# Reordering one DMA queue in a planned attention stage: small moves ahead of bulk loads, residual tiles behind the bias, and other bank tags

## The chip, the cores and the metric

The kernel runs on one core of one Trainium2 chip. The metric is device time in microseconds (us); lower is better. Engines: TensorE (PE), VectorE (DVE), ScalarE (ACT), GpSimd (POOL), and SyncE (SP), which here only issues DMAs.

## The reference, cut to what matters

A two-layer bidirectional encoder is applied to two groups of tokens, 512 and 256 long, 768 columns in all, with a model width of 1024. Layer 0 mixes tokens by windowed attention (16 query heads, 4 key heads, blocks of 128 queries, a bias from relative positions, a sink logit per head):

```
qkv = h @ w_qkv
logits = einsum('bqgrd,bkgd->bgrqk', qb, kb) * scale + band_bias
m = max(max(logits), sink);  p = exp(logits - m)
probs = p / (sum(p) + exp(sink - m))
x = x + einsum('bgrqk,bkgd->bqgrd', probs, vb) @ w_o
```

Layer 1 mixes by a short gated convolution. After each mixer follow an MLP with squared ReLU, `x + square(relu(h @ w_up)) @ w_down`, and a gated per-layer input, `x + (p[i] @ w_proj) * sigmoid(norm(x) @ w_gate)`. All is float32. The change lies in the attention of layer 0 and in the output projection after it.

## The kernel before, in words

**Products.** Every float32 product is made of three reduced ones: an operand is split into a high part (ScalarE, a rounding copy) and a low part (VectorE, the rest), and high by high, high by low and low by high are summed in PSUM. So each weight block that is loaded into a `wraw` tile is first split by ScalarE (`whi`, L656 in the attention) and VectorE (`wlo`, L660).

**Attention is one list.** `mixer_attention` doesn't issue instructions as it goes. It registers operations (`op`, `first`) with an engine, a cost, what must be finished before (`after`), what must merely have started before (`behind`), and for a DMA the time that its bytes take on a modelled pipe. `Plan.order` then plays this list on the host: five engines with a clock of their own, at each step the engine that can start earliest, and on it, among the operations that are ready, the one with the largest `reach` (the modelled time from it to the end) plus a bonus. Scores and what follows them have a bonus of 10 (`URGENT`) on PE, so other products fill the gaps between them. SP also waits when eight DMAs are under way (`LANES`). An operation is offered only when all that it depends on has been placed. The order that comes out is emitted as it stands, one instruction stream for each engine; on the chip an engine works its stream in order and waits where data is late, whatever the planner thought.

**What goes over SP's queue in attention.** Loads of weights (`fetched`: w_q, w_k, w_v, w_o, the projection and p of layer 1), the residual tiles `xa` (x once more, one tile of 128 x 768 for each of 8 output blocks, `load_part`), stores of a small projection (`pj`), and three kinds of moves:
- query moves: `queries` computes two heads for each of 8 units; ScalarE makes the high part `qh` (L712) and VectorE the low part `ql` (L715), and for each head two DMAs copy the halves into a tile `q` that stacks high and low parts over the 128 partitions. The scores S (L1086, L1087) of the head need both;
- key moves, the same for the keys (`kk<-qh`, `kk<-ql`);
- bias moves: for each of 4 groups of heads, two tiles of four moves each, from a skewed table in DRAM (`load_bias`, `bias<-skew`). Four such tiles exist, so those of group 3 wait until group 1 has read its own.

All DMA issues of the list come from L631. Units 4 and 5 are the queries of group 2, 6 and 7 those of group 3.

**Order around the change.** Groups 0 to 3 are attended one after the other, 6 blocks of 128 queries and 4 heads each: score, reduce with the bias (L1093, VectorE), exponent (L1103, ScalarE), scale, transpose (L1129), split, times the values (O, L1144), join into `heads`. Beside them PE works the query products of the units to come and, once two groups are done, blocks of the output projection (`output_part`, mm<-aos, L680), which VectorE adds into `xa` (L1197). Where the list ends, the rest of the output projection runs in plain order over the 8 output blocks (`PAIRED`, L132), in PSUM banks that `both` draws from a pool with three tags: A (4 banks), B and C (2 each). Without a tag, `fresh` walks the tags in the order C, A, B, A.

Of the kernel before, what the change touches and what calls it, by code (L numbers as in the profile page):

```python
# [50 lines left out]
def trunk_kernel(ctx: ExitStack, tc: tile.TileContext, a: dict, out: bass.AP):  # L51
# [67 lines left out]
    def both(name="mm", tag=None):  # L119

        return [t[:, :H] for t in fresh(name, 2, tag)]
# [348 lines left out]
    class Op:  # L470
        def __init__(self, engine, cost, run, after, behind, tail):
            self.engine, self.cost, self.run, self.tail = engine, cost, run, tail
            self.after, self.behind = after, behind
            self.start = self.reach = None

    class Plan:


        LATE = 6.0
        LANES = 8  # L480
        OWN = {"PE": 0.0, "ACT": 0.13, "DVE": 0.12, "POOL": 0.1, "SP": 0.0}
        OTHER = {"PE": 0.22, "ACT": 0.15, "DVE": 0.14, "POOL": 0.3, "SP": 0.1}

# [53 lines left out]
        def order(self):  # L537
            after = {id(o): 0 for o in self.ops}
            nexts = {id(o): [] for o in self.ops}
            for o in self.ops:  # L540
                for d in o.after + o.behind:
                    nexts[id(d)].append(o)
                after[id(o)] = len(o.after) + len(o.behind)
            known, sorted_ = dict(after), [o for o in self.ops if after[id(o)] == 0]
            for o in sorted_:
                for n in nexts[id(o)]:
                    known[id(n)] -= 1
                    if known[id(n)] == 0:
                        sorted_.append(n)
            for o in reversed(sorted_):  # L550
                tail = o.tail + self.LATE if o.tail is not None else self.OTHER[o.engine]
                o.reach = o.cost + max((n.reach + (tail if o in n.after else 0.0) for n in nexts[id(o)]), default=0.0)
            free = {e: 0.0 for e in self.OWN}
            waiting = {e: [] for e in self.OWN}
            pipe, landings = 0.0, [0.0] * self.LANES

            def offer(o):
                o.ready = max(
                    [self.done(d, o.engine) for d in o.after] + [d.start for d in o.behind], default=0.0
                )  # L560
                waiting[o.engine].append(o)

            for o in self.ops:
                if after[id(o)] == 0:
                    offer(o)
            out = []
            while any(waiting.values()):
                best = None
                for e, os in waiting.items():
                    if os:  # L570
                        t = max(free[e], min(o.ready for o in os), landings[-self.LANES] if e == "SP" else 0.0)
                        o = max((o for o in os if o.ready <= t), key=lambda o: o.reach + o.bonus)
                        if best is None or t < best[0]:
                            best = t, o
                t, o = best
                waiting[o.engine].remove(o)
                o.start = t
                free[o.engine] = t + o.cost
                if o.tail is not None:
                    pipe = max(pipe, t + o.cost + 1.3) + o.tail  # L580
                    o.landed = pipe + 0.3
                    landings.append(o.landed)
                o.seq = len(out)
                out.append(o)
                for n in nexts[id(o)]:
                    after[id(n)] -= 1
                    if after[id(n)] == 0:
                        offer(n)
            assert len(out) == len(self.ops)
            return out  # L590
# [12 lines left out]
    def mixer_attention():  # L603
# [23 lines left out]
        def dma(box, src, n, after=(), uses=(), queue="SP", rate=400e3):  # L627

            def run():
                d, s = src()  # L630
                (nc.sync if queue == "SP" else act).dma_start(d, s)  # L631

            lands = n / rate
            if box is not None and box.op is None:
                return first(box, queue, 0.46, run, after, uses, lands)
            return op(queue, 0.46, run, after, uses, lands=lands)

        def fetched(src):
            n = src.shape[1]
            raw = new("wraw", 3, lambda: wp.tile([P, CH], F32, name="wraw", bufs=3))  # L640
            raw.n = n
            raw.landed = [dma(raw, lambda: (raw.t[:, :n], src), P * 4 * n, uses=())]
            return raw

        def pair_tiles():
# [4 lines left out]
        def prepared(raw, n):  # L650

            w, m = pair_tiles(), raw.n
            w.raw = raw.landed[0]

            def high():
                act.activation(w.t[0][:, :m], raw.t[:, :m], AF.Copy)  # L656
                w.parts = blocks(w.t[0][:, :m], n), blocks(w.t[1][:, :m], n)

            def low():
                dve.tensor_tensor(w.t[1][:, :m], raw.t[:, :m], w.t[0][:, :m].bitcast(F32), ALU.subtract)  # L660

            hi = first(w, "ACT", A(m), high, [raw.landed], [raw.key])
            lo = op("DVE", V(m), low, [hi], [w.key, raw.key])
            w.ready = [hi, lo]
            w.keys = [w.key]
            return w
# [194 lines left out]
        for m in range(KB):  # L861
            t = new("L", BL, lambda: odd.tile([P, 2 * LW], F32, tag="L", name="L", bufs=BL)[:, :T])
# [30 lines left out]
        for o, n in ((0, W0), (W0, SEQS[1])):  # L893
            ps = bank("S", "ss")
# [144 lines left out]
        biases = {}  # L1039
# [19 lines left out]
        xa = {}  # L1059
# [124 lines left out]
                ops = split_op(hi, lo, lambda i=i: heads[g].t[:, i, :], T, hparts[g], [heads[g].key])  # L1184
                aos[2 * g + i] = block_of(hi, lo, ops)

        def load_part(ms):
            for m in ms:
                xa[m] = place(m, "xa", F32)
                xa[m].ready = [dma(xa[m], lambda m=m: (xa[m].t[:], a["x"][m]), 393216)]  # L1190

        def output_part(m, w, n, col=0):
            ops = []
            for ps, o, e, last in halves(w, [aos[k] for k in range(n)], ("mm0", "mm1"), col):

                def run(ps=ps, o=o, e=e):
                    dve.tensor_tensor(xa[m].t[:, o : o + e], xa[m].t[:, o : o + e], ps.t[:, :e], ALU.add)  # L1197

                op("DVE", V(e), run, [last, xa[m].ready], [ps.key, xa[m].key])
# [7 lines left out]
        def second_projected():  # L1207
            ps = [pair(2 + p, "p1", F32R) for p in range(2)]
            part1 = []
            for k in range(2):  # L1210
                raw = fetched(a["p"][1, :, k, :])

                def high(k=k, raw=raw):
                    act.activation(ps[0].t[:, k, :], raw.t[:, :T], AF.Copy)

                def low(k=k, raw=raw):
                    dve.tensor_tensor(ps[1].t[:, k, :], raw.t[:, :T], ps[0].t[:, k, :].bitcast(F32), ALU.subtract)

                if k == 0:
                    h = first(ps[0], "ACT", A(T), high, [raw.landed], [raw.key])  # L1220
                    l = first(ps[1], "DVE", V(T), low, [h], [raw.key, ps[0].key])
                else:
                    h = op("ACT", A(T), high, [raw.landed, h], [raw.key, ps[0].key])
                    l = op("DVE", V(T), low, [h, l], [raw.key, ps[0].key, ps[1].key])
                b = Box()
                b.parts = lambda k=k: [p.t[:, k, :] for p in ps]
                b.ready, b.keys = [h, l], [p.key for p in ps]
                part1.append(b)
            w = prepared(fetched(a["proj"][1, 0]), 2)
            for m in range(KB // 2):  # L1230
                projected(1, m, w, part1, temp("n", "pjs"), ("mm0",), False)

# [13 lines left out]
        load_bias(3)  # L1246
        split_heads(0)
        split_heads(1)
        load_part(range(4))
        group_of_heads(2)  # L1250
        for j in range(2):
            w = prepared(fetched(a["w_o0"][j]), 4)
            for i in range(2):
                output_part(2 * j + i, w, 4, i * P)
        split_heads(2)
        load_part(range(4, KB))
        group_of_heads(3)
        for m in range(4, KB):
            output_part(m, prepared(fetched(a["w_o1"][m - 4]), 6), 6)
        split_heads(3)  # L1260
        with s1:
            with tc.manual_schedule(engines={ET.Activation, ET.PE, ET.DVE, ET.SP, ET.Pool}):
# [4 lines left out]
    xa, aos = mixer_attention()  # L1267
# [1054 lines left out]
    behind, product, w0 = second_inputs(xs0[24:])  # L2322
    w = [weight(a["w_o0"][2], 4)] * 2
    w2 = weight(a["w_o2"], 2, tag="z")
    for i, m in enumerate(PAIRED):
        if i == 1:
            w += [weight(a["w_o0"][3], 4)] * 2
        ps = both()
        if m < KB // 2:
            group2(ps, terms_of(w[m], [p[4:] for p in aos], col=m % 2 * P))  # L2330
        else:
            group2(ps, terms_of(w2, [p[6:] for p in aos], col=(m - 4) * P))
        add(m, ps, xa[m])
        n1.block(m, x(m))
        behind(i)
# [103 lines left out]
```

## Time and profile before

| what | us |
|---|---|
| median of 3 runs (lowest, highest) | 1646.12 (1645.8, 1646.88) |
| the profiled execution | 1647.11 |
| its span, first to last instruction | 1645.3 |
| TensorE busy in it | 1627.5 |
| VectorE busy | 1389.8 |
| ScalarE busy | 920.7 |

The span is that of the instructions; the execution's own time is 1.81 longer, and durations below are all from this one execution. Rows of an engine in order of time give the start, the duration, engine, line, output and input, and in brackets how long the engine sat idle just before and what released it. SPq rows are DMA issues, xN is how many were merged, and their duration is the time in which they were issued. Rows of DMA issues by line end with the size of each and the median time from issue to landing. Rows of a stretch give its length, the busy time of PE, PE's weight loads, VectorE, ScalarE and GpSimd, the granted clock of PE as a share of full speed, the busy share of the DMA engines, and GB/s.

### The profile page before, as it was taken

Reading aid. Unit: us, or ns where it says so; the run is one execution under the profiler, and the core shown is the slowest. Engines: PE = TensorE matmul, PEld = TensorE weight load, DVE = VectorE, ACT = ScalarE, POOL = GpSimd, SP = SyncE. Lnnn points to the kernel's source line nnn. Section 1 sums busy time; section 2 is a strip of 40 time slices with the busy share of each in tenths; the row PEclk is TensorE's granted clock in tenths of the full one; section 3 lists DMA queues with packets and bytes.
Section 4 is the critical chain, followed back from the end, with each engine's and each line's share of the span. In section 5 each row is a group of like instructions: output and inputs, shape, how many; then the busy total and the mean of one; then the engine's idle time right before and its main releaser. Section 6 shows DMA issues by size and latency. Waiting matters only on the chain.

```text
span 1645.3 us, 24138 instructions
## 1 busy us (share of the span) xinstructions
PE 1627.5 (99%) x9371; PEld 1575.4 (96%) x9371; DVE 1389.8 (84%) x2212; ACT 920.7 (56%) x1458; POOL 12.3 (1%) x60
## 2 busy tenths in 40 slices
PE   9999999999999999999999999999999999999998
PEld 7988889999999999999999999999999999999987
DVE  7578987999899989977878888769989989999686
ACT  7378884765555545545654344555545555655465
POOL 0000000000000000000000000000000000000000
PEclk9999999999999999999999999999999999999999
DMA  8745303222221222232311222211222222222332
GB/s 309 193 131 135 107 26 96 93 75 74 68 77 66 76 65 85 70 93 78 116 61 52 77 77 77 78 52 53 76 67 85 67 68 74 78 67 75 118 97 87
DMA packets 47822, 144.80 MB, mean 88 GB/s; under 512 B 6075, under 2 KB 9531, under 8 KB 47708
## 3 DMA queue, kind: packets, MB, share of 16 engines
q1 hardware_dynamic: 47708, 143.27, 27.8%
q8 instruction: 73, 1.20, 0.3%
q14 instruction: 41, 0.34, 0.1%
HBM read 123.85 MB, written 9.96 MB: 81 GB/s over the span
## 4 chain that ended last, share of the span: by engine, by line
PE 90%; DVE 5%; DMA 2%; ACT 2%; issue 1%; SPq 0%; DVEq 0%; POOL 0%; ACTq 0%; POOLq 0%
PE a L464 32%; PE b L464 8%; PE mm L132 8%; PE mm L680 8%; PE d L464 5%; PE c L464 5%; PE p L1474 4%; PE gate L1811 4%; PE B L464 4%; PE C L464 4%; PE gate L132 2%; PE down L1811 2%; PE pt L1129 1%; PE O L1144 1%; PE S L1086 1%
## 5 line engine op out<-in xcount | busy, mean ns | idle before, releaser
L432 ACT ACTIVATE whi<-sum 128x1024 fp32r<-128x1024 f32 x66 | 70.2, 1063 | 253.4 <-PE a L464 251.7
L464 PE MATMUL a<-xs,whi 128*128 128x384 f32 x608 | 118.0, 335 | 1.3 <-DVE y L1592 1.3
L464 PEld LDWEIGHTS a<-xs,whi 128*128 128x128 f32 x608 | 106.4, 188 | 2.3 <-DVE y L1592 2.0
L464 PE MATMUL b<-t,zhi 128*128 128x384 f32 x528 | 106.7, 334 | 0.0
L464 PE MATMUL a<-t,zhi 128*128 128x384 f32 x528 | 106.6, 334 | 0.0
L464 PE MATMUL a<-t,whi 128*128 128x384 f32 x528 | 106.6, 334 | 0.0
L1633 DVE TENSOR_TENSOR x<-x,a 128x384 f32<-128x384 f32 x112 | 62.1, 554 | 51.3 <-PE a L464 51.2
L464 PE MATMUL a<-act,whi 128*128 128x384 f32 x448 | 95.6, 334 | 0.0
L464 PEld LDWEIGHTS a<-t,whi 128*128 128x128 f32 x528 | 92.9, 188 | 0.0
L464 PEld LDWEIGHTS b<-t,zhi 128*128 128x128 f32 x528 | 92.9, 188 | 0.0
L464 PEld LDWEIGHTS a<-t,zhi 128*128 128x128 f32 x528 | 92.9, 188 | 0.0
L432 ACT ACTIVATE zhi<-sum 128x1024 fp32r<-128x1024 f32 x66 | 69.8, 1058 | 38.5 <-DVE sum L408 32.7
L443 DVE TENSOR_TENSOR wlo<-wraw,whi 128x1024 fp32r<-128x1024 f32 x72 | 87.6, 1217 | 0.0
L432 ACT ACTIVATE whi<-wraw 128x1024 fp32r<-128x1024 f32 x72 | 75.7, 1051 | 19.3 <-issue 15.6
L680 PE MATMUL mm<-xs_mix,whi 128*128 128x512 f32 (+1 forms) x320 | 81.4, 341 | 0.0
L443 DVE TENSOR_TENSOR zlo<-sum,zhi 128x1024 fp32r<-128x1024 f32 x66 | 80.3, 1217 | 0.5 <-ACT zhi L432 0.5
L443 DVE TENSOR_TENSOR wlo<-sum,whi 128x1024 fp32r<-128x1024 f32 x66 | 80.4, 1218 | 0.0
L464 PEld LDWEIGHTS a<-act,whi 128*128 128x128 f32 x448 | 79.3, 188 | 0.0
L464 PE MATMUL a<-xs,wlo 128*128 128x384 f32 x304 | 64.9, 334 | 0.0
L464 PE MATMUL b<-t,zlo 128*128 128x384 f32 x264 | 61.1, 335 | 0.7 <-DVE zlo L443 0.7
L464 PE MATMUL a<-t,zlo 128*128 128x384 f32 x264 | 60.9, 334 | 0.0
L464 PE MATMUL a<-t,wlo 128*128 128x384 f32 x264 | 60.9, 334 | 0.0
(391 smaller groups left out, 4480.2 us busy)
## 6 DMA issues: line engine op xcount, KB each, us to landing
wraw<-in_up SPq DMA_DIRECT2D x64, 512.0 KB, 3.4
wraw<-in_down SPq DMA_DIRECT2D x64, 512.0 KB, 3.5
wraw<-in_w_in SPq DMA_DIRECT2D x24, 512.0 KB, 3.4
wraw<-in_gate SPq DMA_DIRECT2D x16, 512.0 KB, 3.5
wraw<-in_w_q SPq DMA_DIRECT2D x8, 512.0 KB, 6.2
wraw<-in_w_out SPq DMA_DIRECT2D x8, 512.0 KB, 3.6
x_in<-in_x SPq DMA_DIRECT2D x8, 384.0 KB, 6.9
pj<-L SPq DMA_DIRECT2D x8, 384.0 KB, 5.7
```

What stands on the lines that cost most here:

```text
L132: pe.matmul(t, lhsT=w, rhs=x[:, o:e], start=first and i == 0 and j == 0, stop=last and i == n - 1 and j == 2)
L432: act.activation(hi[:], src, AF.Copy)
L443: dve.tensor_tensor(lo[:], src, hi[:].bitcast(F32), ALU.subtract)
L464: pe.matmul(ps, lhsT=a, rhs=b, start=start and i == 0, stop=i == len(terms) - 1, skip_group_check=True)
L680: pe.matmul(ps.t[:, :n], lhsT=a_, rhs=b_, start=k == 0 and j == 0, stop=k == len(xs) - 1 and j == 2,)
L1086: pe.matmul(S.t[:, :w], lhsT=q, rhs=khh_[g].t[:, kk], start=True, stop=False)
L1129: pe.transpose(pt.t[:, h * P : (h + 1) * P], lg[h // 2].t[:, h % 2, 1 + b * P : 1 + (b + 1) * P], ident[:],)
L1144: pe.matmul(O.t[:], lhsT=vb, rhs=part.t[:], start=b == 0 and i == 0, stop=b == nk - 1 and i == 1)
L1474: pe.matmul(ps[i][o], lhsT=wt[:, c], rhs=xs[f"x{h + 1}{1 + o}"][m][part], start=k == 0 and j == 0, stop=k == KB - 1 and j == 2,)
L1633: dve.tensor_tensor(t[:, o : o + H], t[:, o : o + H], f, op)
L1811: pe.matmul(ps.t[:, o : o + n], lhsT=a_, rhs=b_, start=begin and i == 0 and j == 0, stop=end and i == len(terms) - 1 and j == 2,)
```

## The change

1. Operations get a flag `bulk`. It is set on the loads of p and of the projection of layer 1, on the loads of w_o (`w_o0`, `w_o1`) and on the residual tiles. When the planner would start a bulk operation on SP and another one there, not bulk, is ready within `HOLD` = 2.0 us, it takes the one of these that is ready first, and SP waits for it.
2. The residual tiles 0 to 3 must start behind the last bias move of group 3.
3. The output projection after the list takes its banks by the tags B, A, C, A in turn, not by the walk C, A, B, A.

```diff
@@ class Op / class Plan
-            self.after, self.behind = after, behind
+            self.after, self.behind, self.bulk = after, behind, False
...
         LANES = 8
+        HOLD = 2.0
@@ Plan.order
                         o = max((o for o in os if o.ready <= t), key=lambda o: o.reach + o.bonus)
+                        if o.bulk:
+                            soon = [u for u in os if not u.bulk and u.ready <= t + self.HOLD]
+                            if soon:
+                                o = min(soon, key=lambda u: u.ready)
+                                t = max(t, o.ready)
                         if best is None or t < best[0]:
                             best = t, o
@@ mixer_attention
-        def fetched(src):
+        def fetched(src, bulk=False):
...
+            raw.landed[0].bulk = bulk
             return raw
...
-        def load_part(ms):
+        def load_part(ms, behind=()):
             for m in ms:
                 xa[m] = place(m, "xa", F32)
                 xa[m].ready = [dma(xa[m], lambda m=m: (xa[m].t[:], a["x"][m]), 393216)]
+                xa[m].ready[0].bulk = True
+                xa[m].ready[0].behind.extend(behind)
...
-                raw = fetched(a["p"][1, :, k, :])
+                raw = fetched(a["p"][1, :, k, :], True)
...
-            w = prepared(fetched(a["proj"][1, 0]), 2)
+            w = prepared(fetched(a["proj"][1, 0], True), 2)
...
-        load_part(range(4))
+        load_part(range(4), biases[3][1].ready[-1:])
         group_of_heads(2)
         for j in range(2):
-            w = prepared(fetched(a["w_o0"][j]), 4)
+            w = prepared(fetched(a["w_o0"][j], True), 4)
...
         for m in range(4, KB):
-            output_part(m, prepared(fetched(a["w_o1"][m - 4]), 6), 6)
+            output_part(m, prepared(fetched(a["w_o1"][m - 4], True), 6), 6)
@@ after attention
-        ps = both()
+        ps = both(tag="BACA"[i % 4])
```

## The prediction

> **What bounds the kernel now.** I read the page first, then who waited for whom on TensorE in the first 420 us (attention and what follows it; the diff touches nothing later), then TensorE in order of time around each wait, then the DMA queue of SyncE (SP) beside it, and last a table of stretches for the granted clock and the DMA rate.
>
> ```profile
> span 1645.3 us, 24138 instructions
> PE 1627.5 (99%) x9371; PEld 1575.4 (96%) x9371; DVE 1389.8 (84%) x2212; ACT 920.7 (56%) x1458; POOL 12.3 (1%) x60
> PE S L1086 <- DMA q<-ql: 4.0, 3, 2.3
> PE mm L132 <- DVE xa L1197: 0.6, 1, 0.6
> 153.45 0.40 PE L1144 MATMUL O<-pl,vv 128*128 128x512 f32 x1
> 156.11 0.35 PE L1086 MATMUL S<-kk,q 128*128 128x256 f32 x1 [2.27 <-DMA q<-ql]
> 167.57 0.36 PE L1086 MATMUL S<-kk,q 128*128 128x256 f32 x1 [0.69 <-DMA q<-ql]
> 207.37 0.39 PE L1086 MATMUL S<-kk,q 128*128 128x256 f32 x1 [1.02 <-DMA q<-ql]
> ```
>
> TensorE (PE) is busy 99% of the span, so the list can only give back PE's own idle time. In attention that is nearly all of one kind: three scores (S) wait 2.27, 0.69 and 1.02 us (4.0 in all) for the low part of their queries, which a DMA copies into place. Everything else PE does there is filler without gaps, and the residue of the projection (L680, then L132) runs on after the last head, so that an idle microsecond saved comes off the end. The next rows are the DMA issues of SP around the three waits, the landing times of a few, and the clock.
>
> ```profile
> 146.46 1.10 SPq L631 DMA_DIRECT2D q<-qh  x2
> 147.65 0.53 SPq L631 DMA_DIRECT2D wraw<-in_w_o  x1
> 148.28 1.10 SPq L631 DMA_DIRECT2D q<-ql  x2
> 149.47 1.08 SPq L631 DMA_DIRECT2D xa<-in_x  x2
> 150.64 10.02 SPq L631 DMA_DIRECT2D bias<-skew  x8
> 160.76 1.11 SPq L631 DMA_DIRECT2D q<-qh  x2
> 161.96 0.54 SPq L631 DMA_DIRECT2D wraw<-in_w_o  x1
> 162.60 1.10 SPq L631 DMA_DIRECT2D q<-ql  x2
> ...
> 201.17 0.54 SPq L631 DMA_DIRECT2D wraw<-in_w_o  x1
> 201.80 1.10 SPq L631 DMA_DIRECT2D q<-ql  x2
> ...
> q<-ql SPq DMA_DIRECT2D x2, 192.0 KB, 7.9
> q<-ql SPq DMA_DIRECT2D x2, 192.0 KB, 5.5
> kk<-ql SPq DMA_DIRECT2D x4, 192.0 KB, 4.2
> ...
> L680 PE MATMUL mm<-aos,whi x160: 277/387/481, 188.1 to 261.6; 128*128 128x512 f32 x80, 128*128 128x256 f32 x80
> L1197 DVE TENSOR_TENSOR xa<-xa,mm x16: 410/548/689, 193.4 to 262.1; 128x512 f32<-128x512 f32 x8, 128x256 f32<-128x256 f32 x8
> ...
> 156.10:157.00 0.90, 0.89 (x6) 0.85 (x7) 0.27 (x1) 0.00 (x0) 0.00 (x0) 1.00 0.95 307
> 157.00:158.00 1.00, 1.00 (x8) 0.90 (x7) 0.65 (x3) 0.90 (x1) 0.00 (x0) 0.69 1.10 224
> 158.00:159.00 1.00, 1.00 (x5) 0.90 (x4) 0.38 (x1) 0.98 (x3) 0.00 (x0) 0.50 1.09 197
> 160.00:161.00 1.00, 1.00 (x6) 0.96 (x5) 1.00 (x2) 1.00 (x5) 0.55 (x1) 0.60 0.44 103
> 161.00:162.00 1.00, 1.00 (x6) 0.82 (x5) 0.96 (x4) 0.60 (x3) 0.28 (x2) 1.00 0.53 152
> ```
>
> Before all three waits a load of w_o (512 KB, or 384 KB later) was put on the queue between the high and the low part of the queries. Low parts so placed land 7.9 and 5.5 us after their issue (first and third wait); the low parts of the keys, four with no load among them, land in 4.2. And right after the longest wait the granted clock falls (the column before the DMA share): 0.69, 0.50, 0.50 and 0.60 in the slices from 157 to 161, so 0.31 + 0.50 + 0.50 + 0.40 = 1.71 us of PE's time lost, the slice 159 to 160 being like its neighbour.
>
> **The change part by part.** It adds no instruction and removes none: it reorders SP's list, and gives the banks of eight output tiles other tags. Where the planner's list matters I worked its arithmetic by hand on the list of the kernel before, for order alone and for no time.
>
> *Loads give way (HOLD).* A bulk load now steps back if another SP operation is ready within 2 us on the planner's clock. In each of the three places the low part of the query is already planned when the load is chosen, and ready 0.5 to 0.7 later: it goes first. The scores don't move up in PE's list, since the query products beside them still outrank them by a hair (57.7 to 57.6 at the first). So PE comes to the first score at 153.45 + 0.40 = 153.85 as before. The low parts now issue where the load was, 147.65 and about 148.2, and land by 148.2 + 4.2 = 152.4: **-2.27**, with 1.4 to spare. At the third, 201.17 + 4.2 = 205.4, against 207.37 - 1.02 = 206.35: **-1.02**. The displaced w_o loads come 1.1 us later and are used by products that start at 188.1 (the row of mm<-aos), so nothing waits for them.
>
> *The clock.* The half-speed stretch begins 1 us after the 2.27 us wait, and the waits of 1.02 and 0.69 draw none. I take it as owed to that wait: **-1.71**. Its bounds are 0 and -1.71. The Trainium skill (TensorE: Matmul & The Clock Gate, Part 1, "What's actually happening") says that the clock is halved after an idle window of about 3.4 us; by that rule a 2.27 us wait is too short to be the cause, the loss would stay, and the sum below would be 1.71 us higher. The trace shows a stretch of that length but after a shorter wait, so I let the trace decide and keep the rule as a rival.
>
> *Residual tiles behind the bias.* Two of xa's tiles leave an earlier place, two the place at 149.47; all four now follow the start of the last of the eight bias moves of group 3. They are first added to at 193.4 (L1197), so their own lateness costs nothing. By the planner's clock these start from 145.7 to 148.9, the four tiles from 149.3 to 150.7, and the high part of the next queries (unit 5) starts on ScalarE only at 150.9. HOLD sees nothing that isn't planned, so all four tiles, 1536 KB, go straight ahead of unit 5's moves, for which the second score waits. PE comes to this score at: 167.57 - 0.69 - 156.11 = 10.77 us after the first, less 1.71 at full clock, 9.06; so 153.85 + 9.06 = 162.9, and 163.6 if the planner slips one filler of 3 matmuls (0.68) in front; I take 163.2. On the queue between the first low parts (152.4) and unit 5's first low part lie 512 (w_o) + 768 (bias) + 1536 (xa) + 384 (high) + 192 KB = 3392 KB, 3.47 MB.
>
> ```profile
> 0.00:20.00 20.00, 18.04 (x80) 14.19 (x80) 13.70 (x22) 14.86 (x22) 0.70 (x6) 1.00 0.91 337
> DMA packets 412, 1.07 MB, mean 267 GB/s; under 512 B 64, under 2 KB 64, under 8 KB 412
> 161.10:166.90 5.80, 5.78 (x30) 4.78 (x28) 3.07 (x8) 1.10 (x3) 0.18 (x2) 1.00 0.84 225
> ```
>
> The last column of the stretches is GB/s; the middle row is that of 199 to 203 us, where xa's other four tiles, query moves and a w_o load share the engines, and is the nearest. At 337, 267 and 225 GB/s the 3.47 MB take 10.3, 13.0 and 15.4 us: the low part lands at 162.7, 165.4 or 167.8, and the second wait is 0, 2.2 or 4.6 us. I take 2.2: **+1.5** on the 0.69 of before, between -0.69 and +3.9. That stays just under the 2.27 that drew the clock.
>
> *The early loads of p.* Two query moves and nine bias moves that are ready now pass the first load of p.
>
> ```profile
> 51.82 0.58 SPq L631 DMA_DIRECT2D wraw<-in_p  x1
> 54.02 8.69 SPq L631 DMA_DIRECT2D bias<-skew  x9
> SPq L631 <- DMA wraw<-in_p: 2.7, 2, 1.6
> wraw<-in_p SPq DMA_DIRECT2D x1, 384.0 KB, 7.7
> wraw<-in_p SPq DMA_DIRECT2D x1, 384.0 KB, 4.2
> 59.59 0.85 ACT L1214 ACTIVATE p<-wraw 128x768 fp32r<-128x768 f32 x1 [8.54 <-DMA wraw<-in_p]
> 64.13 1.06 ACT L656 ACTIVATE whi<-wraw 128x1024 fp32r<-128x1024 f32 x1 [3.69 <-PE mm L680]
> 73.11 0.35 PE L1086 MATMUL S<-kk,q 128*128 128x256 f32 x1
> ```
>
> Those eleven ended at 54.02 + 8.69 = 62.7; without p's own issue (0.6) and SP's 2.7 us of waiting for its landing, p is issued at about 59.4, and with 4.2 (its second load, less crowded) it lands at 63.6. ScalarE splits it in 0.85, to 64.4, ahead of the weight split that began at 64.13: **+0.3**, since the score at 73.11, which hangs on what follows, has nothing to spare. The cover of ScalarE's long wait (8.54 at no cost to PE) is thus gone. Bounds: 0 if p lands by 63.2, and the late end is the third rival below.
>
> *Banks.* Tags of the new pool get banks in order of first use, so B, first now, takes the two that C had, and the scores' banks don't come into it; also the first product waited for the last residual add (0.6 us), though the bank it writes had been read earlier: the whole old pool is released at once. **0**, with -0.6 as the other end, if only the banks counted.
>
> *Sum.* -2.27 - 1.02 - 1.71 + 1.5 + 0.3 = -3.2 us. The profiled execution took 1647.11 (span 1645.3 and 1.8 around it), 1.0 over the median of the runs, so it would give 1643.9; the runs, 1646.12 - 3.2 = **1642.9**.
>
> **The rivals.** *The tiles do no harm*: they are drained in time, or the planner lets unit 5's moves pass. Then the second wait goes too, -0.69 in the place of +1.5: 1640.7. For it: SP also loses the waits that stretch its eight bias moves to 10.02 us. Against: the bytes above.
>
> *The clock loss stays*, by the skill's rule or because the second wait, a tenth of a microsecond short of 2.27, draws it anew: 1642.9 + 1.71 = 1644.6. For it: the estimate is so near; against: the waits of about 1 us drew nothing.
>
> *Slower: p comes too late.* ScalarE works in order, so a late p holds the weight split, unit 1's query split and with it the score at 73.11. At worst p is issued at 62.7 and takes its own crowded 7.7: 70.4, and 71.3 after the split, 7.1 us past 64.13, all of it idle PE, long enough to halve the clock for 1.71 more: 1642.6 + 8.8 = 1651.4. It decides from a landing after about 66.5, where it eats the whole gain. The Trainium skill (DMA: Bandwidth & Descriptors, "Rules for kernel authors") asks to issue a DMA early and wait late, which speaks for this rival; the early p of before, waited for at no cost, agrees with it.
>
> **How the numbers follow.** The forecast has 0.37, the harmless tiles 0.24, the clock that stays 0.18, the late p 0.21. 0.2% (3.3 us), about what a measurement of this kernel can tell from no change, puts the border at 1642.8, on the forecast itself: half of its chance counts as faster, half as the same. Faster: 0.18 + 0.24 = 0.42. Same: 0.19 + 0.18 = 0.37. Slower: 0.21. The range goes from just below the harmless case, 1640.4, to 1649.5, which takes in the second wait at its late end with the clock lost (1642.9 + 2.4 + 1.71 = 1647.0) and a late p in part, and leaves out the rest of that rival. Its likely part is 1640.7 to 1644.6.
>
> **What would show it.** Right: query moves in pairs, high then low, with w_o behind; no S wait near 154 and 206; a clock of 1.00 from 150 to 170; four xa issues right after the eight bias moves, and one S wait of about 2 us near 163; p issued near 59 and its split on ScalarE at 63 to 64; L132's first wait still 0.6. The sum is wrong if a score waits over 4 us, if ScalarE's split of p begins after 66, or if PE idles between 60 and 145, where it had no wait of weight.

## The result and the profile after

The changed kernel takes 1649.56 us (median of 20 runs, 1646.48 to 1652.76), the kernel before 1646.86 beside it: ratio 1.0016, 95% interval 1.0010 to 1.0022, 2.7 us slower. The forecast was 3.2 us faster; the median lies 0.06 us above the range. One execution of the kernels below (residual tiles free) took 3888.67 us, far outside all others, and counts in no ratio or mean clock.

The profiled execution of the changed kernel took 1647.17, which is near the fast end of its runs; the profile of before took 1647.11. The first two lines are from its page, the next four from the list of who waited for whom on TensorE up to 420 us (total, times, longest).

```profile
span 1645.4 us, 24132 instructions
PE 1626.4 (99%) x9371; PEld 1574.8 (96%) x9371; DVE 1389.2 (84%) x2212; ACT 920.4 (56%) x1458; POOL 12.6 (1%) x60
```

```profile
PE S L1093 <- DMA q<-ql: 5.5, 2, 3.9
...
PE mm L132 <- DVE xa L1206: 0.6, 1, 0.6
```

The scores' waits for low parts grew from 4.0 to 5.5, in two places instead of three. TensorE in order of time shows where (the brackets hold the wait; line numbers have moved by up to 9):

```profile
74.51 0.36 PE L1093 MATMUL S<-kk,q 128*128 128x256 f32 x1 [1.60 <-DMA q<-ql]
...
164.27 0.28 PE L687 MATMUL mm<-xs_mix,wlo 128*128 128x256 f32 x1
168.42 0.36 PE L1093 MATMUL S<-kk,q 128*128 128x256 f32 x1 [3.87 <-DMA q<-ql]
...
263.18 0.94 PE L132 MATMUL mm<-aos,whi 128*128 128x384 f32 x4 [0.60 <-DVE xa L1206]
```

There is no wait near 154 or 206 any more. The wait at 74.51 is new, and that at 168.42 was 0.69. SP's issues ahead of both:

```profile
59.98 0.35 SPq L637 DMA_DIRECT2D wraw<-in_p  x1
66.44 1.11 SPq L637 DMA_DIRECT2D q<-qh  x2
67.65 0.53 SPq L637 DMA_DIRECT2D wraw<-in_p  x1
68.46 1.10 SPq L637 DMA_DIRECT2D q<-ql  x2
...
147.55 1.10 SPq L637 DMA_DIRECT2D q<-qh  x2
148.94 1.10 SPq L637 DMA_DIRECT2D q<-ql  x2
150.10 0.58 SPq L637 DMA_DIRECT2D wraw<-in_w_o  x1
151.54 5.09 SPq L637 DMA_DIRECT2D bias<-skew  x8
156.73 1.79 SPq L637 DMA_DIRECT2D xa<-in_x  x4
158.62 1.11 SPq L637 DMA_DIRECT2D q<-qh  x2
159.82 1.53 SPq L637 DMA_DIRECT2D q<-ql  x2
161.40 0.64 SPq L637 DMA_DIRECT2D wraw<-in_w_o  x1
```

At group 2's queries the pairs stand as the change wants them, with w_o behind. At unit 1 (66 to 69) the second load of p now stands whole between high and low part. Last, the DMA rate and the clock:

```profile
152.00:168.40 16.40, 12.55 (x75) 10.62 (x74) 10.35 (x24) 8.36 (x20) 1.87 (x4) 1.00 0.93 243
```

```profile
169.00:170.00 1.00, 1.00 (x7) 0.84 (x6) 0.63 (x3) 0.38 (x1) 0.00 (x0) 0.88 0.03 12
170.00:171.00 1.00, 1.00 (x5) 1.00 (x4) 0.79 (x3) 0.82 (x4) 0.00 (x0) 0.50 0.06 16
171.00:172.00 1.00, 1.00 (x4) 0.81 (x3) 0.96 (x6) 0.72 (x3) 0.00 (x0) 0.50 0.00 0
172.00:173.00 1.00, 1.00 (x4) 0.90 (x4) 0.47 (x2) 1.00 (x4) 0.00 (x0) 0.50 0.02 8
173.00:174.00 1.00, 1.00 (x6) 0.96 (x6) 0.88 (x3) 0.55 (x2) 0.00 (x0) 0.92 0.00 0
```

The half-clock stretch did not go: it moved from 157 to 169, behind the longer wait, and costs 0.12 + 0.50 + 0.50 + 0.50 + 0.08 = 1.70 us, as before. From the last row of TensorE above, the end of the list, both kernels take the same time to the end of the span (1382.2 us here; before 1645.3 - 262.65 = 1382.65, from the next row). So the start of that product measures what attention cost.

```profile
262.65 0.94 PE L132 MATMUL mm<-aos,whi 128*128 128x384 f32 x4 [0.60 <-DVE xa L1197]
```

### The profile page after: what moved, and what is told of

It is laid out like the page before. It is cut to its first block, busy times and chain, and to the rows that moved or that the text cites. A ratio compares the mean times of both kernels' runs of the same rounds, so it can differ in the third digit from the quotient of the medians.

```text
span 1645.4 us, 24132 instructions
## 1 busy us (share of the span) xinstructions
PE 1626.4 (99%) x9371; PEld 1574.8 (96%) x9371; DVE 1389.2 (84%) x2212; ACT 920.4 (56%) x1458; POOL 12.6 (1%) x60
## 4 chain that ended last, share of the span: by engine, by line
PE 92%; DVE 5%; ACT 1%; DMA 1%; issue 1%; DVEq 0%; ACTq 0%
PE a L464 32%; PE b L464 8%; PE mm L132 8%; PE mm L687 7%; PE d L464 5%; PE c L464 5%; PE p L1483 4%; PE gate L132 4%; PE gate L1820 4%; PE B L464 4%; PE C L464 4%; PE down L1820 2%; PE O L1151 1%; PE pt L1136 1%; DMA q<-ql 1%; PE S L1093 1%
```

## The experiments

My theory after this reading: the change removes two waits and makes two longer ones, one by the early loads of p (the second load between high and low part), one by the four residual tiles put straight ahead of unit 5's moves; and any long wait draws a half-clock stretch. Rival 1: the loss sits elsewhere in the reordered list or in the banks. Rival 2: the half clock is not owed to the waits. The first four kernels take the two suspects away, one by one and together; they share one chip and the same runs of the kernel before (median 1647.69).

**The changed kernel again.**

> The changed kernel as it stands, beside the three that follow on the same chip. Theory: it loses 1.5 us in waits of scores (3.87 + 1.60 against 4.0 before) and about 1 us in granted clock, because the 3.87 us wait draws a half-clock stretch in every run and the wait of 2.27 us before did not in all: +2.7 us to the kernel before. Rival (order elsewhere): the same +2.7, with the loss in places that have nothing to do with the scores.

1649.70 us, ratio 1.0014 (1.0005 to 1.0023). This execution was profiled at its median, so it is the better picture of the +2 us.

```profile
PE S L1093 <- DMA q<-ql: 6.4, 2, 4.6
...
PE mm L687 <- DVE vv L1038: 0.4, 1, 0.4
```

```profile
75.61 0.36 PE L1093 MATMUL S<-kk,q 128*128 128x256 f32 x1 [1.79 <-DMA q<-ql]
...
265.01 0.94 PE L132 MATMUL mm<-aos,whi 128*128 128x384 f32 x4 [0.60 <-DVE xa L1206]
```

The list ends at 265.01, 2.36 us later than before, and the scores waited 6.4 - 4.0 = 2.4 longer. A wait of 0.4 for the values' split (vv) is new as well. Up to the end of the list TensorE stood idle for 9.73 us against 6.90 before, 2.83 more, and its busy time is 0.47 less (255.28 against 255.75), which makes the 2.36.

**Residual tiles not put behind the bias.**

```diff
-        load_part(range(4), biases[3][1].ready[-1:])
+        load_part(range(4))
```

> The changed kernel, its residual tiles not put behind the bias. Theory: the 3.87 us wait of the score near 168 falls to under 1 and with it goes the half-clock stretch behind it (1.71); the wait of 1.60 near 74 stays. Against the kernel before: -4.0 + 1.6 + 0 to 0.7 for the rest, -1.71 for the clock: -3.4 to -4.1 us, near 1643. Rival 1 (the slow-down sits elsewhere in the list or in the banks): +1 to +3 us as the changed kernel. Rival 2 (the half-clock stretch is not owed to the waits): -1.7 to -2.4 us, mean clock as before.

1646.40 us, ratio 0.9991 (0.9982 to 1.0000): 3.3 under the changed kernel.

```profile
68.90 0.51 PE L687 MATMUL mm<-xs_mix,whi 128*128 128x256 f32 x2 [1.39 <-DVE vv L1038]
76.06 0.36 PE L1093 MATMUL S<-kk,q 128*128 128x256 f32 x1 [1.25 <-DMA q<-ql]
...
166.77 0.36 PE L1093 MATMUL S<-kk,q 128*128 128x256 f32 x1 [1.77 <-DMA q<-ql]
```

The second wait fell from 4.58 to 1.77, not under 1 as expected: two tiles are still on the queue there. The half-clock stretch is gone. The gain on the kernel before was expected at 3.4 to 4.1 and came to about 1.3 to 1.5: the waits here sum to 1.39 + 1.25 + 1.77 = 4.41 against 4.0 before, so in the profiles only the clock is won. The 1.39 for the values' split is the wait that showed with 0.42 in the run above; all of these have the first load of p behind the bias moves. Rival 1 is out (it gave +1 to +3). Rival 2 gave a time near the measured one; one profile without a stretch doesn't settle it, and it is taken up below.

**Loads of p ordinary again.**

```diff
-                raw = fetched(a["p"][1, :, k, :], True)
+                raw = fetched(a["p"][1, :, k, :])
```

> The changed kernel, but the two early loads of p are ordinary loads again and so give way to nothing. Theory: the wait of 1.60 near 74 goes, the 3.87 near 168 stays with its half-clock stretch: 1.6 us under the changed kernel, +1 us against the kernel before, 1647 to 1648. Rival 1 (elsewhere): no change to the changed kernel, +2.7. Rival 3 (it is the 1.60 us wait that draws an additional half-clock stretch in many runs): 1.6 + up to 1.7 under the changed kernel, -0.6 against the kernel before.

1647.48 us, ratio 0.9999 (0.9991 to 1.0008): 2.2 under the changed kernel, about the 1.79 and the 0.42 of the two waits there.

```profile
167.34 0.55 PE L1093 MATMUL S<-kk,q 128*128 128x256 f32 x1 [4.32 <-DMA q<-ql]
```

No wait is left near 74 or 68, and the wait near 163 with its half clock stays (0.91 from 160 to 180, as in the changed kernel). Rival 3 of the expectation, that the shorter wait draws a stretch of its own, has no support: there was one stretch in attention with it and one without.

**Both of these.**

> Both of these: residual tiles not behind the bias, loads of p ordinary; the rest of the change as it is. Theory: no score waits over 0.7 us in attention, no half-clock stretch from 60 to 250 us: -4.0 + 0 to 0.7 for the waits and -1.71 for the clock against the kernel before, -5.0 to -5.7 us, 1640.5 to 1642. Rival 1 (elsewhere): +1 to +3 us. Rival 2 (half clock not owed to the waits): -3.3 to -4.0 us with the mean clock as before.

1642.63 us, ratio 0.9974 (0.9963 to 0.9984), 7.1 under the changed kernel.

```profile
73.45 0.36 PE L1093 MATMUL S<-kk,q 128*128 128x256 f32 x1 [0.17 <-DMA q<-ql]
...
163.63 0.35 PE L1093 MATMUL S<-kk,q 128*128 128x256 f32 x1 [0.91 <-DMA q<-ql]
...
258.59 0.93 PE L132 MATMUL mm<-aos,whi 128*128 128x384 f32 x4 [0.61 <-DVE xa L1206]
```

The list ends 4.1 us earlier than before (262.65 - 258.59), and the profile has no half-clock stretch in attention. The working: 4.58 + 1.79 + 0.42 in waits of the changed kernel against 0.91 + 0.17 is -5.7, and -1.7 for the clock makes -7.4; measured -7.1. So the two suspects and the clock cover all of the loss, and what is left of the change gains 4.3 us on the kernel before by the ratio. Rival 1 is out.

For rival 2 the granted clock that is listed for each execution says more than one profile. It is a mean over the span, and takes in the last microseconds, in which TensorE has no work left and a low clock costs nothing (0.50 over the last 6 us in the profile of the version with both).

| kernel | executions | mean of the listed clocks |
|---|---|---|
| before | 30 | 0.9981 |
| changed, again | 11 | 0.9966 |
| p ordinary | 11 | 0.9968 |
| tiles free | 10 | 0.9982 |
| both of these | 8 | 0.9984 |

The clock falls with the wait of over 4 us behind the four tiles, with and without the wait near 74, and recovers when the tiles are free. So rival 2 is out. But the two kernels whose profiles each show one stretch differ by 0.0015, which is some 2.5 us of 1648 (an estimate from these means): over all its executions the changed kernel loses more clock than the kernel before. In which places, the profiles don't show.

The next four ask how the tiles' place sets the second wait, and what the parts do alone (kernel before: 1646.68).

**Residual tiles behind unit 5's low part** (on top of ordinary loads of p).

```diff
+        last_q = [qst[10].ready[-1], qst[11].ready[-1]]
...
-        load_part(range(4), biases[3][1].ready[-1:])
+        load_part(range(4), last_q)
```

> The changed kernel with the loads of p ordinary and the residual tiles put behind the low part of unit 5's queries instead of behind the bias: no tile (0 KB of xa) stands ahead of that low part. Theory (bytes on the queue ahead of the low part set the wait: four tiles gave 4.32, two gave 0.91, that is 1.7 us a tile): the wait near 163 is 0, no half-clock stretch in attention, 5 to 6 us under the kernel before, up to 0.9 under the version whose tiles are not put behind anything. Rival (the wait of 0.91 that was left is owed to the bias moves and not to the tiles): 0.9 is still there. Rival 2: the tiles now come late for the adds that start near 193 and a wait appears on VectorE or TensorE there.

1641.24 us, ratio 0.9965 (0.9952 to 0.9977): 5.4 us under the kernel before. This is the best version.

```profile
156.63 1.11 SPq L637 DMA_DIRECT2D q<-qh  x2
158.36 1.11 SPq L637 DMA_DIRECT2D q<-ql  x2
159.52 1.57 SPq L637 DMA_DIRECT2D xa<-in_x  x3
```

```profile
160.00:180.00 20.00, 20.00 (x123) 17.70 (x124) 16.32 (x50) 15.83 (x41) 1.01 (x4) 1.00 0.35 113
```

TensorE is busy from 160 to 180 without a gap at full clock; no score waits for a DMA anywhere. The rival that the remaining 0.91 was owed to the bias moves falls, and so does the one of late tiles: no wait appeared for them.

**Three of the four tiles behind the bias.**

```diff
-        load_part(range(4), biases[3][1].ready[-1:])
+        load_part(range(1))
+        load_part(range(1, 4), biases[3][1].ready[-1:])
```

> As the version whose loads of p are ordinary, with three of the four residual tiles behind the bias in place of four (the first goes earlier). Theory: 1.7 us less than four tiles' 4.32, a wait of 2.6 us near 163, long enough for a half-clock stretch behind it, as the 2.27 of the kernel before drew one: 4.0 - 2.6 = 1.4 us under the kernel before, about 1646. Rival (the clock needs a longer idle time; 2.27 was not the cause): no half-clock stretch near 165, 3.1 us under the kernel before.

1646.52 us, ratio 0.9996 (0.9987 to 1.0005).

```profile
166.29 0.36 PE L1093 MATMUL S<-kk,q 128*128 128x256 f32 x1 [4.04 <-DMA q<-ql]
```

A miss: 4.04, not 2.6. My 1.7 us a tile counted the wait, but the wait is a difference of two moving times. Counted from the first high part's issue, the low part ends TensorE's wait after 16.5 us with two tiles on the queue, 20.0 with three and 21.3 with four, so 1.3 to 3.5 a tile (the four being those of the version with ordinary loads of p, the two those of "Both of these"); TensorE itself is there after 15.6, 15.9 and 17.0, since the planner's order differs, and that hid most of the fourth tile. (Of the two, one stands ahead of the bias and not behind it.) The direction holds, the rate for a tile does not. The half-clock stretch is there behind the wait (0.50 from 168 to 170), so the rival is out.

**The tiles behind the bias alone**, on the kernel before, no load giving way.

```diff
-        load_part(range(4))
+        load_part(range(4), biases[3][1].ready[-1:])
```

> The kernel before with one part of the change alone: four residual tiles behind the first bias moves of group 3, no load gives way. The load of w_o stays between high and low part. Theory: first wait 2.27 less some tenths (two tiles no longer stand in the queue there), the second rises from 0.69 by two tiles' 1.7 each to about 4, with a half-clock stretch each: 2 to 4 us over the kernel before. Rival (tiles cost only together with moves in pairs): second wait stays under 1.5 and the time is that of the kernel before within 1 us.

1647.11 us, ratio 1.0002 (0.9993 to 1.0011).

```profile
155.30 0.35 PE L1086 MATMUL S<-kk,q 128*128 128x256 f32 x1 [1.39 <-DMA wraw<-in_w_o]
169.44 0.36 PE L1086 MATMUL S<-kk,q 128*128 128x256 f32 x1 [2.93 <-DMA q<-ql]
```

The second wait rose as expected in kind, less in size (2.93, not 4: the planner mixed the four tiles among the bias moves); but the first fell to 1.39 and drew no stretch, the third (1.02 before) does not show, and the stretch came behind the second. (For the first wait the profile names the load of w_o, which the score doesn't read; it names what came last.) The parts balance: no difference, where I had expected 2 to 4 us.

**The banks alone**, on the kernel before.

```diff
-        ps = both()
+        ps = both(tag="BACA"[i % 4])
```

> The kernel before with the tags of the eight output tiles alone changed. Theory: nothing, 0 +- 0.5 us; the first product of the rest still waits 0.6 us for the last residual add. Rival (the banks count): that wait goes, -0.6 us, or the first products wait longer for the scores' banks and it is slower by the 1 to 2.7 us that the changed kernel lost.

1647.44 us, ratio 0.9999 (0.9990 to 1.0008): nothing, and the product still waits 0.60 for the last residual add. The run gives something else, because its attention is that of the kernel before:

```profile
156.07 0.35 PE L1086 MATMUL S<-kk,q 128*128 128x256 f32 x1 [1.64 <-DMA q<-ql]
167.04 0.36 PE L1086 MATMUL S<-kk,q 128*128 128x256 f32 x1 [1.52 <-DMA q<-ql]
206.85 0.39 PE L1086 MATMUL S<-kk,q 128*128 128x256 f32 x1 [1.03 <-DMA q<-ql]
262.08 0.93 PE L132 MATMUL mm<-aos,whi 128*128 128x384 f32 x4 [0.60 <-DVE xa L1197]
```

The same order waited 1.64 at the first score in this execution and 2.27 in the profile of before, and here no stretch followed.

The last three take the best version apart (kernel before: 1646.40).

**The second load of p alone gives way.**

```diff
-                raw = fetched(a["p"][1, :, k, :])
+                raw = fetched(a["p"][1, :, k, :], k == 1)
```

> The version with ordinary loads of p and residual tiles behind unit 5's low part, but the second of the two early loads of p gives way again: it stands whole between the high and the low part of unit 1's queries, while the first load of p keeps its early place. Theory (the 1.60 us wait near 74 of the changed kernel is owed to the place of the second load): a wait of 1.2 to 1.6 us is there, no wait on the values' split near 68, 3.8 to 4.2 us under the kernel before. Rival (it is owed to the first load, which now comes behind the bias moves): no wait near 74, 5.4 us under the kernel before.

1642.37 us, ratio 0.9974 (0.9965 to 0.9984).

```profile
74.38 0.36 PE L1093 MATMUL S<-kk,q 128*128 128x256 f32 x1 [1.59 <-DMA q<-ql]
```

The wait is there in full, without a wait for the values' split. So it is the second load's place that makes it, and the first load's lateness at most the 0 to 1.4 of that split. The listed clock of these nine executions has a mean of 0.9984, so a wait of this length draws no stretch that shows there.

**Only the loads of w_o give way**, tiles ordinary, banks of before.

```diff
-                xa[m].ready[0].bulk = True
...
-            w = prepared(fetched(a["proj"][1, 0], True), 2)
+            w = prepared(fetched(a["proj"][1, 0]), 2)
...
-        ps = both(tag="BACA"[i % 4])
+        ps = both()
```

> The version with residual tiles behind unit 5's low part, with only the loads of w_o giving way: the tiles, the loads of p and of the projection are ordinary, and the output tiles have the banks of the kernel before. Theory (the rest of the change's flags and the banks do nothing): the same as that version within 0.5 us, 5 to 6 us under the kernel before, all score waits for a DMA gone. Rival (banks, or the tiles' flag): 1 us or more away from it.

1642.62 us, ratio 0.9975 (0.9965 to 0.9986). The median is 1.4 us above that of the best version, which ran on another chip; the intervals of the two ratios overlap, so the time alone doesn't tell them apart. The trace does:

```profile
190.29 1.10 SPq L637 DMA_DIRECT2D q<-qh  x2
191.48 1.05 SPq L637 DMA_DIRECT2D xa<-in_x  x2
192.63 1.10 SPq L637 DMA_DIRECT2D q<-ql  x2
```

```profile
199.61 0.36 PE L1093 MATMUL S<-kk,q 128*128 128x256 f32 x1 [1.83 <-DMA q<-ql]
```

Two of the later tiles (4 to 7), no longer bulk, slip between high and low part of the next queries, and the score behind them waits 1.83. The tiles' flag keeps such a wait away, where my theory said that it does nothing; its worth in time isn't settled, since the flag of the projection and the banks went with it.

**The tiles behind unit 5's low part alone**, on the kernel before.

```diff
+        last_q = [qst[10].ready[-1], qst[11].ready[-1]]
...
-        load_part(range(4))
+        load_part(range(4), last_q)
```

> The kernel before with its residual tiles behind unit 5's low part and nothing else: the loads of w_o stay between high and low parts. Theory: first wait 1.6 to 2.3 and third 1.0 stay, the second (0.7 to 1.5) goes, the half-clock stretch behind the first stays in the runs that have it: 0.7 to 1.5 us under the kernel before; what the loads of w_o giving way is worth is then the remaining 4 us. Rival (the tiles' place alone makes the gain): 4 to 5.4 us under the kernel before.

1644.93 us, ratio 0.9992 (0.9983 to 1.0001), about 1.5 under the kernel before.

```profile
154.76 0.36 PE L1086 MATMUL S<-kk,q 128*128 128x256 f32 x1 [1.26 <-DMA wraw<-in_w_o]
165.97 0.36 PE L1086 MATMUL S<-kk,q 128*128 128x256 f32 x1 [1.75 <-DMA q<-ql]
205.77 0.39 PE L1086 MATMUL S<-kk,q 128*128 128x256 f32 x1 [1.03 <-DMA q<-ql]
```

The time came as expected, but not by the expected step: the second wait did not go. With w_o between high and low part it is 1.75, and the three waits sum to 4.04 as against 3.98 before. The interval takes in no change, and where the 1.5 us would lie is not shown: this profile has no half-clock stretch in attention, but the means of the listed clocks are alike (0.9982 here, 0.9983 before). All three waits need the loads to give way; with that, the best version is some 4 us faster than this one, each against its own runs.

The main versions together, each against its own runs of the kernel before (the first row is the three runs that the prediction had):

| kernel | median | ratio (95%) | scores' waits for DMA in the profile | half-clock stretch behind one |
|---|---|---|---|---|
| before | 1646.12 | 1 | 2.27, 0.69, 1.02 | yes |
| changed | 1649.56 | 1.0016 (1.0010 to 1.0022) | 1.60, 3.87 | yes |
| changed, again | 1649.70 | 1.0014 (1.0005 to 1.0023) | 1.79, 4.58 | yes |
| tiles free | 1646.40 | 0.9991 (0.9982 to 1.0000) | 1.25, 1.77 | no |
| p ordinary | 1647.48 | 0.9999 (0.9991 to 1.0008) | 4.32 | yes |
| both of these | 1642.63 | 0.9974 (0.9963 to 0.9984) | 0.17, 0.91 | no |
| p ordinary, tiles behind unit 5 | 1641.24 | 0.9965 (0.9952 to 0.9977) | none | no |

## Why the prediction was wrong, step by step

**Loads give way: right.** The waits near 154 and 206 are gone, 2.27 and 1.02, with the pairs in the forecast order and no wait for the displaced loads of w_o.

**The early loads of p: the step that failed.** It followed the first load alone, and that one well: issued at 59.98 for the forecast 59.4, and split from 63.52 as the forecast said (63 to 64). The second load, from the same line in the loop over two, was used for its landing time and never moved. It stood between the two high parts of unit 1 and now stands behind both, straight ahead of the low parts; HOLD could not see these, since they were not placed yet when the load was chosen. I had stated this blind spot for the residual tiles and did not apply it here, though the prediction named an idle TensorE between 60 and 145 as a sign that the sum is wrong. The price is 1.59 to 1.79, and the version with the second load alone shows it. The first load's +0.3 was also the low end, and came another way: not over ScalarE's weight split but over VectorE, where the low part of p (L1226) goes ahead of the values' split. The split of p began at 63.52, 64.42 and 65.40 in three executions, and the wait for the values was 0, 0.42 and 1.39.

**The residual tiles: right in mechanism, a term mis-sized.** The wait came where the bytes were said to put it, at 3.87 to 4.58 in place of 2.2, inside the stated bound of 4.6. Of the two times in it, TensorE's was right: 164.27 + 0.28 is 1.35 later than 163.2, about what the new wait near 74 had added. The low part landed at 168.4, not at 165.4. The start near 152.4 held: the first low parts were issued at 148.94, later than taken, but landed in 3.3 us in place of 4.2. What was off is the rate, 243 GB/s in the measured stretch against the 267 taken (1.3 us), and the byte count: the load of w_o issued at 161.40, right behind the low parts, was left out (0.39 MB, 1.6 us). With it the 3.47 are 3.86 MB, 15.9 us at 243 GB/s, and 152.4 + 15.9 = 168.3.

```profile
q<-ql SPq DMA_DIRECT2D x2, 192.0 KB, 8.6
wraw<-in_w_o SPq DMA_DIRECT2D x1, 384.0 KB, 8.5
```

These are the issues of 159.82 and 161.40. The load landed 1.5 us behind the low part, but from 168.4 to 170.0 the DMA engines moved only some 0.06 MB (37 GB/s), so most of the load had moved by the time that the low part landed. That the wait would be shorter without it is argued from the sum and was not tried.

**The clock: the cause right, the term wrong twice.** The stretch belongs to long waits: with all of them gone it goes too, and the listed clocks agree. But -1.71 needed every wait to stay short, and the forecast's own 2.2 lay on the edge, as its second rival said; the wait was longer, and the stretch moved behind it. And the kernel before does not always have it: the same order waited 1.64 and drew none in the run with other banks. What one profile shows of it is one execution's draw: the kernel before has a mean listed clock of 0.9981 to 0.9983 in three sets of 22 to 30 executions, 0.0001 to 0.0003, or 0.2 to 0.5 us, under the 0.9984 of the 40 executions of the five versions in which the loads of w_o give way and no score's wait is over 1.83 us. By this estimate, from clocks rounded to 0.001, most of the 1.71 was not there to be won in the median execution from which it was taken off. The rule of the Trainium skill (TensorE: Matmul & The Clock Gate, Part 1, "What's actually happening"), by which an idle window of about 3.4 us halves the clock, does not give these rows as a bound on the wait: waits of 2.27 and 2.93 drew a stretch.

**Banks: right**, nothing: the product after the list waits 0.60 as before.

**The sum.** By the steps, with the measured sizes of the run at the median: the old waits -2.27 - 0.69 - 1.02, the new 4.58 + 1.79 + 0.42, and 0 for the clock, +2.8; TensorE's busy time gave back 0.47, the list ended 2.36 later and the medians differ by 2.0 to 2.7. This is the sum of two profiled executions. Over all executions the clock is no 0 but some 2.1 to 2.5 us against the kernel before (mean listed clock 0.9968 over the 20 runs of the result and 0.9966 over the 11, against 0.9981), so how the loss divides between longer waits and clock in an average execution stays open. **The rivals.** The slower one was a late first p, which did not happen; the kernel is slower by the second p and by the tiles, whose late end I had as a bound for 1647.0, together with the clock, but not with a second new wait.

## What to carry to other kernels

When a rule moves every load of a kind, walk each load it touches and name the small move that now stands straight behind it; a planner that lets ready work pass cannot see work that it has not placed. For the bulk loads here the place that cost nothing was behind the last urgent move, not ahead of it: the same four tiles made a wait of over 4 us on one side of the query moves and none on the other. Count the loads that follow close behind too when you size a queue's landing, keep waits short of the length that halves the clock, since such a wait is paid for twice, and don't take a clock loss seen in one profile off the median of many runs.

## What the hardware showed that I had not expected

In attention, 16 score waits from 0.69 to 1.83 us in the profiles of these kernels were not followed by a half-clock stretch of their own, and all six of 2.27 us and more (2.27, 2.93, 3.87, 4.04, 4.32, 4.58) had one, with about 1.7 us lost. So the edge lies between 1.83 and 2.27 in these profiles, one execution of each kernel; whether it is sharp they don't show. The waits themselves vary between executions of one order: 2.27 and 1.64 at the same score, 3.87 and 4.58 at another.
